# A hand-written order on TensorE: scores and conditioning chunks moved between a tile's transpositions and its value products

## Chip, cores and metric

The kernel runs on one core of one Trainium2 chip. The metric is the device time of one launch in microseconds (us). The engines are TensorE (PE in the profile, with its weight loads as PEld), VectorE (DVE), ScalarE (ACT), GpSimd (POOL) and SyncE (SP, which here only issues the loads of weights). Each engine works through its own list of instructions in the order of that list.

## What is computed

A model of two layers on 256 tokens of width 1024. Layer 0 mixes with a gated linear recurrence, layer 1 with an attention of three branches; each layer ends with a gated feed-forward part, and every part is scaled and shifted by columns computed from a conditioning vector `c`. The change lies in layer 1. Cut to what matters:

```python
mods = einsum('bd,lde->lbe', silu(c), ada_w) + ada_b        # shift, scale, gate of four parts
kc, vc = compress(k_cmp), compress(v_cmp)                   # silu(flat @ w1) @ w2, kc then normalised
q = rms_norm(h @ w_q, q_norm); q_rope = apply_rope(q)
o_c = softmax(mask(q @ kc)) @ vc                            # compressed branch
o_s = softmax(mask(q_rope @ ks)) @ vs                       # selected branch
o_w = softmax(mask(q_rope @ kw)) @ vw                       # window branch
y = (g0 * o_c + g1 * o_s + g2 * o_w) @ w_out
x = x + gate * y
```

## The kernel before

Weights come as 1 MB chunks in the fixed order `SCHED`, over the SP queue into four buffers (`raw`). A chunk of a projection is split by ACT (`wh`) and DVE (`wl`) into a high and a low part, and TensorE multiplies three times per product (`mm3`). A conditioning chunk (`ada_pe`, products `adapsg` for a gate, `adapsss` for shift and scale) is read by TensorE straight from `raw`. A buffer is loaded again once its reader is done.

The attention of layer 1 (`nsa`) is written as units, generators that issue some instructions and yield. `ORDER["nsa"]` is a list of their names; each word lets one unit go on to its next yield:

- `q0` to `q3`: a query projection (`nq`), then its rotation, for which four small transfers (`usq`) are issued from the ACT queue. `n0`, `n1`, `n2`: the norm of a pair of query chunks or of the keys: sums on TensorE (`hs`), a chain of small steps over ACT and DVE (`hry`, `hrt`, `hrr`), products that spread the result (`hb`), and the scaling on DVE (`QR`, `QN`).
- `c`: the compression, whose tail (`cmp_tail`) is a chain of small steps: transpositions (`hidt`), products (`kc`, `kcms`, `vc`), with DVE steps between. `G`: gates. `w0`, `w1`: the values (`v`). `x0`, `x1`: compressed softmax (`cs`, `css`, transposed as `pct` to `PC`).
- For each head tile j from 0 to 7: `s` (`attend_scores`) makes scores `s` on TensorE, DVE adds the mask and takes maxima into `Pt`, ACT takes eight exponentials in place, and DVE scales `Pt`. `p` (`attend_turns`) transposes `Pt` on TensorE into `ptt`, and DVE (one of four) and ACT (three of four) copy it to `PT`. `v` (`attend_values`) makes the output `po` from `PT` and the values, and ACT and DVE split it to `hh` and `hl`.
- `a`: the next conditioning chunk, of twelve: four of the gate of the attention, eight for the last feed-forward part. After the last chunk of each group ACT copies the sum (`adasm`), TensorE transposes it (`adat`), and DVE adds the bias.

In this stretch TensorE keeps exactly the order in which the units write (`InOrder` ties each product to the one before it). ACT and DVE are ordered by the scheduler from the dependences. Score tiles, `po`, `hb`, `adat` and other small results share four PSUM buffers (`m_tile`) taken in turn; `ptt` and the projections share three others (`acc_tile`). `Pt` has three buffers. After the attention come the output projection (`nso`), the second feed-forward part (`ff`, `ffo`), and the end.

Of the kernel before, what the change touches and what calls it, by code (L numbers as in the profile page):

```python
# [52 lines left out]
def _ada_g(l):  # L53
# [12 lines left out]
    "hada": [1, 1, 3, 4, 6, 6, 6, 7, 7, 7, 8, 8],  # L66
    "f0": [11, 11, 12, 12, 13, 17, 19, 20, 20, 20, 25, 25, 26, 27, 29, 30, 32, 33, 35, 36],
    "nsa": (
# [3 lines left out]
    ).split(),  # L72
    "f1": [15, 16, 24, 29],
}
# [151 lines left out]
class K:  # L226
# [177 lines left out]
    def ada_pe(self, kind, l, i, t):  # L404

        nc = self.nc
        ss = kind == "ss"
        q = 512 if ss else 256
        if i == 0:
            self.aps = self.pp.tile([P, 512], F32, tag="ada", bufs=1, name=f"adaps{kind}{l}")  # L410
        ks = [i] if ss else [2 * i, 2 * i + 1]
        last = i == (7 if ss else 3)
        for n, k in enumerate(ks):
            for j in range(4):
                self.pe.matmul(self.aps[32 * j:32 * j + 32, :q], lhsT=self.c32[:, k],
                                 rhs=t[:, n * D + j * q:n * D + (j + 1) * q], start=k == 0, stop=k == KD - 1,
                                 tile_position=(0, 32 * j))
        if not last:
            return
        m, A, bias = self.ada_tiles(l)  # L420
        nb = q // P
        sm = self.tp.tile([P, 512], F32, tag="junk", bufs=1, name="adasm")
        nc.scalar.copy(sm[:, :q], self.aps[:, :q])
        pt = self.m_tile([P, 4, P], "adat")
        for b in range(nb):
            self.pe.transpose(pt[:, b, :], sm[:, b * P:(b + 1) * P], self.c("ident"))
        lo, hi = (0, 16) if ss else (16, 24)
        nc.vector.tensor_tensor(m[:, lo:hi].rearrange("p (j b) -> p j b", b=nb),
                                pt.rearrange("p b (j r) -> p j b r", r=32)[:, :, :nb, 0],
                                bias[:, lo:hi].rearrange("p (j b) -> p j b", b=nb), op=ALU.add)  # L430
        if ss:
            nc.vector.scalar_tensor_tensor(A, m[:, 8:16], 1.0, self.col(self.gain(l)), op0=ALU.add, op1=ALU.mult)
            self.mods[("A", l)] = A
            self.mods[("shift", l)] = m[:, 0:8]
        else:
            self.mods[("gate", l)] = m[:, 16:24]
# [592 lines left out]
    def nsa(self):  # L1029
        nc = self.nc  # L1030
        with self.tc.tile_pool(name="ns", bufs=1) as sp, self.tc.tile_pool(name="ns2", bufs=2) as s2, \
# [85 lines left out]
            for t in ORDER["nsa"]:  # L1117
                n = int(t[1:] or 0)
                if t == "a":
                    self.adas(1)  # L1120
                    continue
                if t[0] == "v" and self.O is None:
                    self.O = self.h_tiles(0)
                if (t[0], n) not in units:
                    units[t[0], n] = make[t[0]](n)
                next(units[t[0], n], None)
# [351 lines left out]
```

## Time and profile before

| | |
|---|---|
| time, median of 3 runs | 772.63 us (771.39 to 773.84) |
| the profiled execution | 770.48 us, of which its span is 768.7 us |
| TensorE busy | 718.0 us, 93% of the span |
| DVE, ACT busy | 568.6 us (74%), 399.7 us (52%) |
| mean granted TensorE clock | 0.991 of full |

The span runs from the first to the last instruction of the profiled execution; the rest of its time lies around it. Busy times overlap between engines, and products are pipelined, so the idle time of an engine and what ended it say more than its busy share.

### The profile page before, as it was taken

Reading aid. Unit: us, or ns where it says so; the run is one execution under the profiler, and the core shown is the slowest. Engines: PE = TensorE matmul, PEld = TensorE weight load, DVE = VectorE, ACT = ScalarE, POOL = GpSimd, SP = SyncE. Lnnn points to the kernel's source line nnn. Section 1 sums busy time; section 2 is a strip of 40 time slices with the busy share of each in tenths; the row PEclk is TensorE's granted clock in tenths of the full one; section 3 lists DMA queues with packets and bytes.
Section 4 is the critical chain, followed back from the end, with each engine's and each line's share of the span. In section 5 each row is a group of like instructions: output and inputs, shape, how many; then the busy total and the mean of one; then the engine's idle time right before and its main releaser. Section 6 shows DMA issues by size and latency. Waiting matters only on the chain.

```text
span 768.7 us, 15837 instructions
## 1 busy us (share of the span) xinstructions
PE 718.0 (93%) x6548; PEld 663.5 (86%) x6548; DVE 568.6 (74%) x1167; ACT 399.7 (52%) x758; POOL 0.4 (0%) x5
## 2 busy tenths in 40 slices
PE   4999998899999999999998787878999999999997
PEld 2999976799999999999997766544699999999997
DVE  6996988378998979888697796664489758565531
ACT  4339877356635454545476545355476544444330
POOL 0000000000000000000000000000000000000000
PEclk9999999999999999999999998999999999999999
DMA  8999646457397978987545722026965555755710
GB/s 335 335 353 352 253 154 278 170 190 254 117 371 292 364 282 336 350 300 287 178 147 193 285 70 69 1 110 238 359 240 203 187 198 212 256 202 208 267 42 22
DMA packets 26571, 174.13 MB, mean 227 GB/s; under 512 B 3201, under 2 KB 4609, under 8 KB 6018
## 3 DMA queue, kind: packets, MB, share of 16 engines
q1 hardware_dynamic: 24912, 170.80, 60.0%
q10 hardware_dynamic: 1586, 2.32, 1.1%
q8 instruction: 51, 0.84, 0.4%
q14 instruction: 22, 0.18, 0.1%
HBM read 170.48 MB, written 1.05 MB: 223 GB/s over the span
## 4 chain that ended last, share of the span: by engine, by line
PE 79%; DVE 9%; ACT 6%; DMA 3%; issue 2%; ACTq 0%; DVEq 0%
PE ff L516 11%; PE ff L514 11%; PE ff L515 11%; PE ffo L514 6%; PE ffo L515 5%; PE ffo L516 5%; ACT Pt L459 3%; DVE wl L338 2%; PE po L220 1%; DVE Pt L1300 1%; PE s L220 1%; PE hg_g L514 1%; PE hg_i L796 1%; PE nso L514 1%; PE q L515 1%
## 5 line engine op out<-in xcount | busy, mean ns | idle before, releaser
L338 DVE TENSOR_TENSOR wl<-raw,wh 128x1024 fp32r<-128x1024 f32 x201 | 243.7, 1221 | 75.3 <-ACT wh L337 74.5
L337 ACT CAST wh<-raw 128x1024 fp32r<-128x1024 f32 x201 | 208.3, 1048 | 146.3 <-PE ff L515 53.0
L516 PE MATMUL ff<-hh,wl 128*128 128x256 f32 (+1 forms) x704 | 198.5, 282 | 0.0
L514 PE MATMUL ff<-hh,wh 128*128 128x256 f32 (+1 forms) x704 | 198.2, 282 | 0.0
L515 PE MATMUL ff<-hl,wh 128*128 128x256 f32 (+1 forms) x704 | 197.7, 281 | 0.0
L516 PEld LDWEIGHTS ff<-hh,wl 128*128 128x128 f32 x704 | 133.1, 189 | 0.0
L514 PEld LDWEIGHTS ff<-hh,wh 128*128 128x128 f32 x704 | 132.7, 189 | 0.3 <-ACT hh L550 0.2
L515 PEld LDWEIGHTS ff<-hl,wh 128*128 128x128 f32 x704 | 132.6, 189 | 0.0
L514 PE MATMUL ffo<-gh,wh 128*128 128x256 f32 x352 | 99.0, 282 | 0.6 <-DVE x L668 0.6
L515 PE MATMUL ffo<-gl,wh 128*128 128x256 f32 x352 | 98.6, 280 | 0.0
L516 PE MATMUL ffo<-gh,wl 128*128 128x256 f32 x352 | 98.5, 280 | 0.0
L389 DVE CUSTOM_DVE_ANT_0 junk<-raw,crep 128x1024 f32<-128x1024 f32 x64 | 78.0, 1219 | 1.3 <-DMA raw<-in_w 0.6
L514 PEld LDWEIGHTS ffo<-gh,wh 128*128 128x128 f32 x352 | 66.0, 188 | 1.3 <-DVE x L668 1.0
L516 PEld LDWEIGHTS ffo<-gh,wl 128*128 128x128 f32 x352 | 66.1, 188 | 0.0
L515 PEld LDWEIGHTS ffo<-gl,wh 128*128 128x128 f32 x352 | 66.1, 188 | 0.0
L509 ACT CAST gh<-fg 128x256 fp32r<-128x256 f32 x44 | 17.8, 405 | 41.5 <-DVE fg L957 40.9
L459 ACT ACTIVATE Pt<-Pt,nm 128x128 f32<-128x128 f32 x64 | 28.2, 443 | 18.1 <-DVE nm L1304 18.1
L510 DVE TENSOR_TENSOR gl<-fg,gh 128x256 fp32r<-128x256 f32 x44 | 18.5, 421 | 8.2 <-ACT gh L509 8.2
L617 ACT ACTIVATE hh<-t,mod 128x256 fp32r<-128x256 f32 x24 | 11.4, 505 | 24.0 <-DVE t L616 24.0
L459 ACT ACTIVATE fs<-ff 128x256 f32<-128x256 f32 x38 | 14.4, 380 | 14.9 <-PE ff L516 14.8
L668 DVE SCALAR_TENSOR_TENSOR x<-ffo,mod,x 128x256 f32<-128x256 f32 x16 | 7.7, 481 | 19.1 <-PE ffo L516 19.1
L220 PE MATMUL nq<-hh,wl 128*128 128x256 f32 x64 | 18.7, 292 | 1.0 <-DVE wl L338 1.0
(323 smaller groups left out, 1446.7 us busy)
## 6 DMA issues: line engine op xcount, KB each, us to landing
raw<-in_w SPq DMA_DIRECT2D x160, 1024.0 KB, 5.9
x<-in_x SPq DMA_DIRECT2D x2, 512.0 KB, 4.9
usq<-huq ACTq DMA_DIRECT2D x16, 64.0 KB, 2.0
out<-x SPq DMA_DIRECT2D x8, 128.0 KB, 2.1
cst<-in_cst ACTq DMA_DIRECT2D x1, 558.0 KB, 7.6
raw<-in_w SPq DMA_DIRECT2D x1, 512.0 KB, 3.5
usk<-huk ACTq DMA_DIRECT2D x8, 64.0 KB, 2.6
rselr<-in_rsel SPq DMA_DIRECT2D x1, 256.0 KB, 2.8
```

What stands on the lines that cost most here:

```text
L220: return self.then(self.k.nc.tensor.matmul(*a, **k))
L337: nc.scalar.copy(wh, u)
L338: nc.vector.tensor_tensor(wl, u, wh.bitcast(F32), op=ALU.subtract)
L389: nc.vector.tensor_tensor_reduce(out=junk, in0=t[:, h * D:(h + 1) * D], in1=self.crep, scale=1.0, scalar=0.0, op0=ALU.mult, op1=ALU.add, a ...
L459: r = nc.scalar.activation(out, in_, func, **kw)
L509: self.nc.scalar.copy(hi, v)
L510: self.nc.vector.tensor_tensor(lo, v, hi.bitcast(F32), op=ALU.subtract)
L514: mm(ps, lhsT=wh, rhs=hh, start=first, stop=False)
L515: mm(ps, lhsT=wh, rhs=hl, start=False, stop=False)
L516: return mm(ps, lhsT=wl, rhs=hh, start=False, stop=last)
L617: self.last_hh = nc.scalar.activation(hh[:, m, :256], t, AF.Identity, bias=sh[:, m:m + 1])
L668: nc.vector.scalar_tensor_tensor(xn[:, m], ps, gate[:, m:m + 1], xn[:, m], op0=ALU.mult, op1=ALU.add)
```

## The change

The list `ORDER["nsa"]` is written anew, and the tail of a conditioning group (`ada_cols`) becomes a word of its own, `A`.

```diff
     "nsa": (
-        "q0 q0 q0 q0 n2 c G G c G q1 q1 q1 c q1 c w0 w0 c c n0 w0 w0 q2 q2 q2 q2 n0 s0 s0 x0 s1 s1 q3 q3 x0 q3 q3 "
-        "s2 s2 n1 w1 w1 w1 w1 n1 p0 p0 v0 s3 s3 p1 p1 v1 s4 s4 x1 p2 p2 v2 s5 s5 a a x1 p3 p3 v3 s6 s6 a a p4 p4 v4 "
-        "s7 s7 a a a p5 p5 v5 a a p6 p6 v6 a a a p7 p7 v7"
+        "q0 q0 q0 q0 n2 c G G c G q1 q1 q1 q1 w0 w0 c w0 w0 n0 c q2 q2 c c q2 q2 n0 s0 s0 x0 s1 s1 q3 q3 q3 q3 s2 s2 "
+        "x0 n1 w1 w1 w1 w1 p0 p0 a n1 v0 s3 s3 p1 p1 s4 s4 v1 x1 p2 p2 s5 s5 v2 a x1 p3 p3 s6 s6 v3 a p4 p4 s7 s7 v4 "
+        "a A a p5 p5 a v5 a a p6 p6 a a v6 a a p7 p7 A v7"
     ).split(),
...
-        if not last:
-            return
+        if last and isinstance(self.pe, InOrder):
+            self.ada_tail = lambda: self.ada_cols(l, ss, q)
+        elif last:
+            self.ada_cols(l, ss, q)
+
+    def ada_cols(self, l, ss, q):
+        nc = self.nc
         m, A, bias = self.ada_tiles(l)
         nb = q // P
...
                 if t == "a":
                     self.adas(1)
                     continue
+                if t == "A":
+                    self.ada_tail()
+                    continue
```

On TensorE, the second norm of the queries. Before, its eight `hb` products (the last two are shown) follow the products of the values (`v`) directly, and the first tile's transpositions (`ptt` from `Pt`) and value products (`po`) come after them:

```order
L220 MATMUL hb<-hry,rsel 128x256
L220 MATMUL hb<-hrt,rsel 128x256
L223 MATMUL ptt<-cst,Pt_5727 128x128 x12
L220 MATMUL po<-PC_5855,VC 64x256 x2
L220 MATMUL po<-PT_10_6028,V 64x256
```

Now the transpositions and a first conditioning chunk stand between the last product of the values and the first two of `hb`:

```order
L220 MATMUL v_5958<-wh_1_5952,hl_5240 128x256
L223 MATMUL ptt<-cst,Pt_5727 128x128 x12
L220 MATMUL adapsg_6032<-raw_5526,c_110 32x256 x8
L220 MATMUL hb<-hry,rsel 128x256
L220 MATMUL hb<-hrt,rsel 128x256
```

So `hb` moved behind two pieces of work that do not need it.

On TensorE, tile 1 (`Pt_5783`). Before, its values (`po`, ten products) follow its transpositions, and the scores come behind:

```order
L223 MATMUL ptt<-cst,Pt_5783 128x128 x12
L220 MATMUL po<-PC_5855,VC 64x256 x2
L220 MATMUL po<-PT_10_6103,V 64x256
L220 MATMUL po<-PT_00_6097,V 64x256
L220 MATMUL po<-PT_10_6103,V 64x128
L220 MATMUL po<-PT_00_6097,V 64x128
L220 MATMUL po<-PT_11_6115,V 64x256
L220 MATMUL po<-PT_01_6109,V 64x256
L220 MATMUL po<-PT_11_6115,V 64x128
L220 MATMUL po<-PT_01_6109,V 64x128
L220 MATMUL s_6138<-KR,QR 128x256
```

Now the scores of tile 4 stand between the two:

```order
L223 MATMUL ptt<-cst,Pt_5783 128x128 x12
L220 MATMUL s_6136<-KR,QR 128x256
L220 MATMUL s_6135<-KR,QR 128x256
L220 MATMUL s_6144<-KR,QR 128x512
L220 MATMUL s_6143<-KR,QR 128x512
L220 MATMUL po<-PC_5927,VC 64x256 x2
L220 MATMUL po<-PT_10_6114,V 64x256
```

The same holds for tiles 2, 3 and 4 with the scores of tiles 5, 6 and 7.

On ACT, the copy `adasm` after the gate's last chunk. Before, it stands behind the last exponential of tile 5 and ahead of the copies of tile 4:

```order
L459 ACTIVATE Pt_6328,sm<-Pt_6328,nm 128x128
L459 ACTIVATE Pt_6328,sm<-Pt_6328,nm 128x256
L423 COPY adasm<-adapsg_6263 128x256
L1338 COPY PT_10_6394<-ptt 128x384
L1338 COPY PT_01_6400<-ptt 128x384
```

Now it stands behind the last exponential of tile 7 and ahead of the copies of tile 5:

```order
L464 ACTIVATE Pt_6398,sm<-Pt_6398,nm 128x128
L464 ACTIVATE Pt_6398,sm<-Pt_6398,nm 128x256
L428 COPY adasm<-adapsg_6032 128x256
L459 ACT_TABLE_LOAD
L1346 COPY PT_10_6474<-ptt 128x384
```

So the copy moved two tiles back on ACT; on TensorE `adat` still follows the gate's last chunk directly.

## Rows read from the trace of the kernel before

**Rows 1.** The page: busy time of each engine, share of the span, instructions.

```profile
PE 718.0 (93%) x6548; PEld 663.5 (86%) x6548; DVE 568.6 (74%) x1167; ACT 399.7 (52%) x758; POOL 0.4 (0%) x5
```

**Rows 2.** Two stretches: length, busy time of each engine, clock, DMA share, GB/s.

```profile
422.00:551.00 129.00, 103.55 (x784) 72.83 (x783) 83.70 (x276) 65.03 (x202) 0.00 (x0) 0.96 0.42 154
551.00:768.70 217.70, 213.71 (x1780) 212.35 (x1779) 136.68 (x205) 98.57 (x148) 0.00 (x0) 1.00 0.53 189
```

**Rows 3.** TensorE's waits, 422 to 551 us: total, times, longest.

```profile
PE po L220 <- ACT PT L1338: 7.0, 4, 2.8
PE adat L223 <- ACT adasm L423: 4.0, 2, 3.3
PE pct L223 <- DVE nm L1304: 3.6, 1, 3.6
PE hb L220 <- ACT hry L509: 3.4, 1, 3.4
PE hidt L223 <- DVE hid L1185: 1.8, 1, 1.8
PE kc L220 <- DVE wd L1203: 1.5, 1, 1.5
...
PE ptt L223 <- ACT PT L1338: 0.8, 3, 0.3
PE hs L220 <- DVE mx L1300: 0.6, 1, 0.6
PE adapsss L220 <- DMA raw<-in_w: 0.6, 1, 0.6
```

**Rows 4.** Waits of DVE and ACT in the same stretch.

```profile
ACT Pt L459 <- DVE nm L1304: 18.1, 6, 4.0
DVE rs L1313 <- ACT Pt L459: 17.9, 7, 3.7
...
DVE usq L1002 <- DMA usq<-huq: 2.5, 1, 2.5
DVE VC L1229 <- PE vc L220: 2.3, 1, 2.3
```

**Rows 5.** Groups by line, 422 to 551 us: busy, mean ns of one, idle before.

```profile
L1300 DVE CUSTOM_DVE_ANT_0 Pt<-s,cst 128x128 f32<-128x128 f32 (+1 forms) x64 | 18.9, 351 | 0.2 <-PE s L220 0.2
L1321 DVE TENSOR_TENSOR Pt<-Pt,cf 128x768 f32<-128x768 f32 x16 | 14.6, 953 | 0.2
L338 DVE TENSOR_TENSOR wl<-raw,wh 128x1024 fp32r<-128x1024 f32 x12 | 14.4, 1214 | 1.7 <-ACT wh L337 1.6
```

**Rows 6.** Instructions of TensorE in order of time: start, us.

```profile
504.00 0.65 PE L220 MATMUL po<-PT,V 128*64 128x256 f32 x4 [2.77 <-ACT PT L1338]
...
522.16 0.44 PE L223 MATMUL adat<-cst,adasm 128*128 128x128 f32 x2 [3.34 <-ACT adasm L423]
...
538.31 1.74 PE L223 MATMUL ptt<-cst,Pt 128*128 128x128 f32 x12
...
549.96 0.87 PE L220 MATMUL po<-PT,V 128*64 128x256 f32 x8
```

**Rows 7.** Four stretches, columns as in Rows 2.

```profile
462.00:464.00 2.00, 2.00 (x10) 2.00 (x10) 1.24 (x2) 2.00 (x11) 0.00 (x0) 0.50 0.16 20
480.00:482.00 2.00, 2.00 (x12) 2.00 (x12) 2.00 (x4) 0.00 (x0) 0.00 (x0) 0.53 0.00 0
504.00:506.00 2.00, 2.00 (x14) 1.15 (x14) 2.00 (x6) 0.37 (x1) 0.00 (x0) 1.00 0.00 0
524.00:526.00 2.00, 2.00 (x10) 1.16 (x11) 0.76 (x3) 1.04 (x3) 0.00 (x0) 0.50 0.57 234
```

**Rows 8.** The chain that ended last, whole run: start, us, what.

```profile
518.24 3.61 ACT Pt L459 x16
...
530.87 2.29 ACT Pt L459 x11
...
536.52 1.04 PE adapsss L220 x8
```

## Prediction

> **What bounds the kernel now.** I read the page first: TensorE is busy for 718.0 of 768.7 us and no other engine comes near [rows 1]. So time can only come out of stretches in which TensorE stands still. The table of stretches shows where: from 422 to 551 us, the attention, it is busy for 103.6 of 129.0 us; from 551 us to the end for 213.7 of 217.7 us [rows 2]. The part behind the attention starts when the attention ends and is then bound by TensorE, so what the attention saves comes off the end at full value. The third view, the waits of TensorE in this stretch, names what is to be had: 25.2 us over thirteen groups, of which the nine that the argument needs are shown [rows 3], and the difference of the two numbers above, 25.4 us, agrees. That is the ceiling for idle time, and the change touches nearly every line of it.
>
> The fourth view says why it can't all go. The largest waits of the other two engines are a pair: ACT waits 18.1 us for DVE's `nm`, and DVE waits 17.9 us for ACT's exponentials [rows 4]. The reader is to see a loop: maxima, exponentials (3.6 us a tile [rows 8]), scaling of `Pt` (2 x 0.95 us), and 8 maxima of 0.35 us each before the next `nm` [rows 5]. Each list is run in order, so a new order on TensorE helps only as far as this loop and the other lists let it.
>
> Finally the clock. After the waits of 3.4 us (`hb`) and 3.3 us (`adat`) the granted clock is 0.53 and 0.50, the 1.2 GHz level, and after that of 3.6 us (`pct`) 0.50, while after one of 2.8 us it is 1.00 [rows 3, 6, 7].
>
> **The change, step by step.** Nothing is added or removed in work: the same products, copies and transfers in another order. I read the new lists of TensorE, ACT and DVE side by side and put the durations of the rows to them. Each term is what TensorE waits before, less what it waits after.
>
> T1, compression's tail. Before, `hidt` and `kc` wait 1.8 and 1.5 us [rows 3]; now 24 products of the values stand ahead of each, and both waits go. But the query norm `n0` and the first scores need DVE's list, and there only the wait for `vc` (2.3 us) goes; that for the transfer `usq` (2.5 us) stays, and waits for ACT come to it [rows 4]. About 2 us of idle time reappear ahead of `hb`. I take 1.0 us of gain; bounds 0 and 3.3.
>
> T2, `pct`. Before, `x0`'s transposition stands 24 query products behind the scores and waits 3.6 us, and `hs` behind it 0.6 us [rows 3]. Now all 48 query products and the scores of tile 2 stand ahead of it, and its softmax is ready. What is late next: the last `wl` of the value weights `w1` stands on DVE behind the maxima of tile 2 and costs 1.2 us [rows 5], and the second dozen value products need it. Gain 4.2 - 1.2 = 3.0 us; bounds 2.0 and 4.2.
>
> T3, `hb` of `n1`. Before it waits 3.4 us for the last step of the chain on ACT and DVE [rows 3]. Now 12 transpositions (1.74 us [rows 6]) and a chunk (1.04 us [rows 8]) stand ahead of it. But on ACT the chain now stands behind the exponentials of tiles 1 and 2, with four issues of `usq` among them, and behind the copy of the values; on DVE it stands behind the scaling of two tiles. The chain comes about 1 us earlier than before, and TensorE, early by T1 and T2 less these 2.8 us, too: the wait stays at about 3.4 us. And the third of the transpositions' four PSUM tiles now waits about 1.2 us for the copy of the values to free a buffer. Net -1.2 us; bounds -1.5 and +3.4 (the chain in time).
>
> T4, the value products of tiles 1 to 4. Before, `po` waits 7.0 us for copies of `ptt`, and `ptt` 0.8 us [rows 3]: ACT runs eight exponentials between the copies. The four score products now ahead of `po` (about 2 us) cover most of this for tiles 1 and 3 and half of it for tile 4. For tile 2 another wait takes its place. The small PSUM tiles go round in fours, so `po` of tile 2 needs the buffer of tile 5's first scores, which DVE reads only after the scaling of tile 4 (2 x 0.95 us) and among eight steps of `x1`: 2.4 us, and 0.9 us ahead of it, where these scores wait for `hl` of tile 1, behind eight exponentials. Sum after: 0.5 + 2.4 + 0.9 + 0.9 + 0.4 = 5.1 us, gain 7.8 - 5.1 = 2.7 us; bounds 0 and 7.
>
> T5, `adat`. Before it waits 3.3 us for `adasm`, behind the exponentials of tile 5 (begun at 518.24, 3.61 us [rows 8]), and 0.7 us at the second group: 4.0 in all [rows 3]. Now `A` follows the last gate chunk with nothing between, and ACT has `adasm` behind the exponentials of tile 7. Their start, by the loop above, is about 517 us, their end 521; TensorE arrives at about 517. I take 4.2 us. The second `A` has 12 transpositions ahead of it and costs nothing. Net -0.2 us; bounds -3 and +4.0. The Trainium skill says in TensorE: Matmul & The Clock Gate, section Architectural detail, that ACT and DVE take their queue strictly in order while TensorE can only pull weight loads ahead. By that rule `adasm` can't overtake the exponentials and the 4.2 us stand; if it could, the sum would be about 4 us better. The trace agrees: 518.24 + 3.61 is 521.85, and `adat` starts at 522.16 [rows 6, 8].
>
> T6, transfers. The first chunk is used at about 473 us in place of 507, so its buffer is loaded again 34 us sooner, and chunks 5 to 12 follow, each one buffer round behind. The last two still come close together with tile 6 and 7, and the output projection's weights queue behind them on SP: I take 1.8 us (1.3 for the last chunk, 0.5 at the first `nso`) against 0.6 before [rows 3]. Net -1.2 us; bounds -3 and +0.6.
>
> T7, the clock. Three slow stretches before, each about 3.4 us at half speed, so about 1.7 us apiece; with `pct` gone two are left (`hb`, `adat`). Gain 1.7 us; bounds 0 and 5.1. The Trainium skill, same page, section HAM oscillation, states that long idle gaps send the array back to half rate and that work must be laid so that it stays warm. By that rule the price hangs on these two waits alone: the 3.4 us still to be had are lost as long as they stay. The rows shown agree with it.
>
> Sum: 1.0 + 3.0 - 1.2 + 2.7 - 0.2 - 1.2 + 1.7 = 5.8 us. A second way, without the ledger: in the new order `adat` and, behind it, eight chunks (8 x 1.04), three tiles of transpositions (3 x 1.74) and of values (3 x about 2 us; the last 8 of 20 rows take 0.87 [rows 6]) and the second `adat` follow the wait that ends at 521.3 us: about 20.5 us, with 1.7 for the clock and 1.3 for the transfer 544.8 us. Before, the last value product ends at 549.96 + 0.87 = 550.83 us [rows 6]: 6.0 us. I take 6.0 us: 770.48 - 6.0 = 764.5 us for the profiled execution. It lies 2.15 us under the median of the runs, so the median becomes 772.6 - 6.0 = 766.6 us. A difference of 0.3%, about 2.3 us, is what a measurement can tell from none.
>
> **The rivals.**
>
> The waits only move. TensorE is ahead of the loop of DVE and ACT, and whatever stands earlier is waited for later: T4 gives 0, T2 2.0, T7 0, the rest as above: 1.0 + 2.0 - 1.2 - 0.2 - 1.2 = 0.4 us. For it: the pair of 18 us [rows 4]. Against: DVE is busy only for 83.7 and ACT for 65.0 of 129 us [rows 2]. Time 772.2 us.
>
> The cover is better than I read. `adasm` is in time, or the chain of `n1` is: either gives 4 to 5 us and its slow stretch of 1.7 us, so 12 us in all: 760.6 us. For it: 2.8 us of work ahead of `hb`. Against: both are behind exponentials on ACT's list.
>
> Slower, by `adat`. It stands between the last gate chunk and everything else that TensorE has left, and behind the exponentials of tile 7 in place of tile 5. If the new order brings these no sooner than before (530.87 us [rows 8]), `adat` starts at 534.8, the 20.5 us behind it end at 555.3 and, with the transfer then in time and the clock as before, 4.5 us are lost: 777.1 us. It decides from a start of about 526 us on; I expect 517. Against: the scores of tiles 3 to 7 all stand earlier among TensorE's products, and the waits of T2 alone move them 3 us.
>
> **How the numbers follow.** The forecast has 0.60, the better cover 0.20, waits that only move 0.13, slower 0.07. The forecast's own bounds, most terms not at their ends at once, are 762 to 770 us. The range to hold 8 in 10 takes in the better cover down to 759.5 and part of the moved waits up to 771.5 us. Faster by over 0.3% (under 770.3): all of the better cover and nearly all of the forecast, 0.79. Same: 0.14. Slower: 0.07.
>
> **What would show it.** T1: no waits at `hidt` and `kc`, one of about 2 us at `hb` of `n0`. T2: none at `pct`, about 1 us inside `v`. T3: `hb` of `n1` starts at about 477 us after 3.5 us, the clock then near 0.5. T4: `po` of tile 2 waits for DVE, not for ACT's copies. T5: one wait of about 4 us at the first `adat` for `adasm`, with exponentials until about 521 us. The end of the last `po` at 544 to 545 us, and a part behind it as long as before. Wrong it would be made by a wait on none of these places, or by an `nso` that starves for weights.

## The result and the profile after

The new order takes 769.02 us, the median of nine runs (766.25 to 772.83), against 774.19 us for the kernel before, run between them (nine runs, 771.39 to 776.76). The ratio is 0.9933, with a 95% interval of 0.9906 to 0.9959: 5.2 us faster, where 6.0 us were forecast. The profiled execution takes 767.16 us (forecast 764.5), its span is 765.4 us.

The page's busy line of the new kernel, which answers to [rows 1]: the work of TensorE is the same, at a lower mean clock (0.984 against 0.991).

```profile
PE 719.0 (94%) x6548; PEld 664.1 (87%) x6548; DVE 567.9 (74%) x1167; ACT 399.0 (52%) x758; POOL 0.4 (0%) x5
```

Two stretches of the new kernel, as in [rows 2]: the attention, and all behind it.

```profile
422.00:545.00 123.00, 102.15 (x762) 71.91 (x762) 81.01 (x271) 62.04 (x200) 0.00 (x0) 0.92 0.43 153
545.00:765.40 220.40, 216.01 (x1802) 213.89 (x1798) 138.58 (x210) 100.45 (x150) 0.00 (x0) 1.00 0.53 192
```

As the prediction has it, the gain lies in the attention; but the granted clock there fell from 0.96 to 0.92, where it should have risen. The waits of TensorE, 422 to 551 us, which answer to [rows 3]:

```profile
PE hb L220 <- ACT hry L514: 5.0, 1, 5.0
PE adat L223 <- ACT adasm L428: 3.8, 1, 3.8
PE vc L220 <- DVE hrt L495: 3.0, 1, 3.0
PE po L220 <- DVE mx L1308: 2.0, 1, 2.0
PE po L220 <- ACT PT L1346: 1.9, 2, 1.0
PE v L220 <- DVE wl L338: 1.1, 1, 1.1
...
PE adapsss L220 <- DMA raw<-in_w: 1.0, 1, 1.0
PE ptt L223 <- DVE PT L1344: 0.8, 2, 0.5
...
PE ptt L223 <- ACT PT L1346: 0.2, 1, 0.2
```

Gone are `pct`, `hidt`, `kc` and most of the wait of `po` for the copies. In their place stand a longer wait of `hb` (5.0 for 3.4), one of `vc` (3.0) that I had put elsewhere, and the forecast ones: `po` for the maxima of tile 2, `wl` inside `v`, the last transfer.

The waits of ACT and DVE, 422 to 545 us, which answer to [rows 4]:

```profile
ACT hh L514 <- PE po L220: 19.5, 6, 6.3
...
ACT Pt L464 <- DVE nm L1312: 6.0, 3, 3.8
...
DVE rs L1321 <- ACT Pt L464: 4.0, 3, 3.4
```

The pair that stood at 18.1 and 17.9 us fell to 6.0 and 4.0 us; ACT now waits most for `po` of TensorE. So the loop of maxima and exponentials, which the prediction takes as the limit of any new order, held this order far less than the old one. Both e1 (13.6 and 14.6 us) and e2 (11.0 and 8.2 us), described below, have part of the fall.

To see where the time went, I cut the attention at a point that both kernels pass with nearly the same work done, the start of tile 3's scores behind `hb`. It begins where the gates are transposed (`gt`) and ends with the last `po`. Each profile has its own start, so lengths are compared. First before, then after, columns as above:

```profile
421.75:484.97 63.22, 50.06 (x365) 43.02 (x365) 49.58 (x136) 31.69 (x87) 0.00 (x0) 0.95 0.38 131
484.97:550.83 65.86, 53.57 (x421) 29.89 (x419) 34.10 (x140) 33.47 (x114) 0.00 (x0) 0.97 0.46 177
```

```profile
421.69:486.10 64.41, 53.02 (x382) 44.07 (x380) 49.34 (x136) 30.74 (x87) 0.00 (x0) 0.89 0.43 145
486.10:546.70 60.60, 51.14 (x403) 29.31 (x401) 33.09 (x139) 33.30 (x114) 0.00 (x0) 0.94 0.46 168
```

The front, up to tile 3's scores, became 1.2 us longer, the back 5.3 us shorter; 1.04 us of each is the one chunk that moved from back to front. Idle time, length less TensorE's busy time, fell from 13.2 to 11.4 us in front and from 12.3 to 9.5 us in the back, 4.6 us in all. Busy time, less the chunk, rose by 1.9 us in front and fell by 1.4 us in the back, though the products are the same. In front that is the clock, 0.89 for 0.95. The fall in the back, at a clock of 0.94 for 0.97, needs another cause; e9 below shows half of it in the scores. The sum, 4.1 us, less 0.8 us that the part behind the last `po` is longer in this profile, is the 3.3 us between the two profiled executions. The medians differ by more, 5.2 us: the profile shown of before is one of its fastest executions (770.48 us at a clock of 0.991, where runs of before have a median near 0.982).

### The profile page after: what moved, and what is told of

Its sections match the earlier page's. It is cut to its first block, busy times and chain, and to the rows that moved or that the text cites. A ratio compares the mean times of both kernels' runs of the same rounds, so it can differ in the third digit from the quotient of the medians.

```text
span 765.4 us, 15842 instructions
## 1 busy us (share of the span) xinstructions
PE 719.0 (94%) x6548; PEld 664.1 (87%) x6548; DVE 567.9 (74%) x1167; ACT 399.0 (52%) x758; POOL 0.4 (0%) x5
## 5 line engine op out<-in xcount | busy, mean ns | idle before, releaser
L622 ACT ACTIVATE hh<-t,mod 128x256 fp32r<-128x256 f32 x24 | 11.4, 505 | 24.4 <-DVE t L621 24.4
L1308 DVE CUSTOM_DVE_ANT_0 Pt<-s,cst 128x128 f32<-128x128 f32 (+1 forms) x64 | 19.4, 351 | 5.6 <-PE s L220 5.6
L464 ACT ACTIVATE fs<-ff 128x256 f32<-128x256 f32 x38 | 14.4, 380 | 14.6 <-PE ff L521 14.6
```

The lines of the kernel that those rows point to most:

```text
L464: r = nc.scalar.activation(out, in_, func, **kw)
L622: self.last_hh = nc.scalar.activation(hh[:, m, :256], t, AF.Identity, bias=sh[:, m:m + 1])
L1308: nc.vector.tensor_tensor_reduce(out=Pt[half][:, br, o:o + n], in0=ps[half][:, br], in1=cs[:, S - n:], scale=1.0, scalar=-3e38, op0=ALU.ad ...
```

## The experiments

Twelve runs, each timed beside the kernel before on the same chip. Except where it is said, the edit is one of the written order alone. The table gives the ratio to before; the median of the mean granted clock over the runs of a kernel (before had 0.979 to 0.982 in these jobs); and from its profile the length from `gt` to the last `po` and TensorE's idle time in it. Filler products count as busy.

| kernel | ratio (95%) | median clock | length | idle |
|---|---|---|---|---|
| before | 1 | 0.979 to 0.982 | 129.1 | 25.5 |
| after | 0.9933 (0.9906 to 0.9959) | 0.982 | 125.0 | 20.9 |
| e1 new front, old back | 1.0033 (1.0007 to 1.0060) | 0.979 | 133.4 | 26.1 |
| e2 old front, new back | 0.9852 (0.9822 to 0.9881) | 0.991 | 122.5 | 19.0 |
| e3 after, old compression tail | 0.9918 (0.9889 to 0.9947) | 0.983 | 122.6 | 21.1 |
| e4 after, `hb` of `n1` later | 0.9825 (0.9799 to 0.9850) | 0.984 | 119.2 | 14.6 |
| e5 e3 and e4 together | 0.9815 (0.9777 to 0.9854) | 0.989 | 119.2 | 15.9 |
| e6 e5, `A` later | 0.9822 (0.9781 to 0.9862) | 0.989 | 117.4 | 15.7 |
| e7 after, filler ahead of `hb` | 0.9879 (0.9845 to 0.9912) | 0.984 | 123.9 | 16.0 |
| e8 after again | 0.9916 (0.9889 to 0.9944) | 0.982 | 128.2 | 21.0 |
| e9 before, scores moved | 0.9894 (0.9858 to 0.9930) | 0.985 | 124.1 | 20.3 |
| e10 before, chunks and `n1` moved | 0.9924 (0.9897 to 0.9951) | 0.985 | 126.6 | 23.2 |
| e11 e5, filler ahead of `adat` | 0.9761 (0.9727 to 0.9795) | 0.995 | 116.2 | 11.5 |
| e12 e5 with the front of before | 0.9805 (0.9772 to 0.9838) | 0.989 | 120.1 | 16.7 |

The ratios are to be trusted first, the idle column second, the length last, since it holds the clock of one execution: the changed kernel, profiled twice (after and e8), has the same idle time, 20.9 and 21.0 us, and the same waits within 0.7 us each, but lengths of 125.0 and 128.2 us.

**Front and back apart.** e1 keeps the new order up to the values (`w1`) and goes back to the old one behind it, the conditioning tail included. e2 is the reverse:

```diff
 e1, behind w1 (the lines of before return):
-p0 p0 a n1 v0 s3 s3 p1 p1 s4 s4 v1 ... v4 a A a p5 p5 a v5 a a p6 p6 a a v6 a a p7 p7 A v7
+n1 p0 p0 v0 s3 s3 p1 p1 v1 s4 s4 ... v4 s7 s7 a a a p5 p5 v5 a a p6 p6 v6 a a a p7 p7 v7
 e2, ahead of w1 (the lines of before return):
-q1 q1 q1 q1 w0 w0 c w0 w0 n0 c q2 q2 c c q2 q2 n0 s0 s0 x0 s1 s1 q3 q3 q3 q3 s2 s2 x0 n1
+q1 q1 q1 c q1 c w0 w0 c c n0 w0 w0 q2 q2 q2 q2 n0 s0 s0 x0 s1 s1 q3 q3 x0 q3 q3 s2 s2 n1
```

> The new order up to the value products w1 (compression's tail and x0 moved), the old one from the first transpositions on. Theory A: the front's savings are eaten by the wait for hb of n1, whose chain on ACT and DVE comes no earlier; so the first scores of tile 3 start within 1 us of before (484.97 us) and the time is that of before within 1.5 us (ratio 0.998 to 1.002). Rival B: the tail and pct give 2 to 4 us that last to the end (ratio 0.995 to 0.997).

> The old order up to w1, the new one from the first transpositions on (scores ahead of the value products, chunks spread, the late A). Theory A: all of the gain of the changed kernel is here, 4 us or more at the end of the last value product, ratio 0.992 to 0.995. Rival B: half of it, ratio 0.996 to 0.998.

Measured: e1 is 0.3% slower than before, e2 1.5% faster, more than either of its expectations had. The front takes from the change rather than adding to it. The longest wait of TensorE in e1, 422 to 551 us:

```profile
PE hb L220 <- ACT hry L509: 7.9, 1, 7.9
```

It was 3.4 us before [rows 3]: the waits removed at `pct` and the compression are all met again here, and at `vc` (2.5 us).

**Which half of the front.** e3 gives the changed kernel the old compression tail back and leaves `x0` where the change put it. It differs from e2 only in the place of `x0`:

```diff
-q1 q1 q1 q1 w0 w0 c w0 w0 n0 c q2 q2 c c q2 q2 n0 s0 s0 x0
+q1 q1 q1 c q1 c w0 w0 c c n0 w0 w0 q2 q2 q2 q2 n0 s0 s0 x0
```

> The changed kernel with the old order of compression's tail (q1 to n0), all else new. Theory A: the new tail gave nothing, since the wait for the transfer usq on DVE decides there; the first scores start at about 448.5 us in place of 449.1, and the time is that of the changed kernel or up to 1 us less (ratio 0.991 to 0.994). Rival: the tail was worth the 3.3 us of its two waits, and the time goes back by 2 to 3 us (ratio 0.996 to 0.998).

Measured: no difference from the changed kernel that the runs can tell (0.9918; after had 0.9933 and, timed again as e8, 0.9916), so the tail is worth nothing that they show either way: `hidt` and `kc` wait 1.8 and 1.5 us again, `vc` no longer waits. Against e2 (0.9852) it is slower, and the intervals do not meet. So what costs is the move of `x0`. The two profiles show this only in part. `hb` waits 4.7 us here and 0.9 us in e2, where `pct` and `hs` wait 3.1 us instead, and the idle times differ by 2.1 us; the lengths are alike, since the profile of e3 is the fastest of its runs and that of e2 the slowest. The rest of the 4.8 us between the medians goes with the clock (0.983 for 0.991), and how `x0` sets that is not shown.

Why `hb` waits longer, the chain that ended last in the changed kernel shows (start, us, what):

```profile
469.62 6.37 DMA usq<-huq
476.11 0.75 DVE usq L1007
476.94 0.65 DVE QR L1008
477.59 1.74 DVE Pt L1329 x2
479.32 0.34 DVE hrt L495
...
480.02 0.43 DVE hrr L498
480.54 0.41 ACT hry L514
480.99 2.32 PE hb L220 x8
```

The chain of `n1` stands on DVE behind `usq` and two scalings of `Pt`, and `usq` is a transfer that took 6.37 us. The view of the tile `usq` gives the time from issue to landing, first for e2, then for e3, 440 to 486 and 440 to 482 us:

```profile
DMA to landing us min/median/max: 2.0/2.0/2.1
```

```profile
DMA to landing us min/median/max: 2.0/3.3/6.5
```

Beside the transfer stands a load of weights, issued on SP's queue (changed kernel, 468 to 475 us):

```profile
468.73 0.33 SPq L317 DMA_DIRECT2D raw<-in_w  x1
```

The four `usq` transfers of 64 KB are issued from ACT's queue at 467.73, 468.34, 468.98 and 469.62 us. The first two landed after 2.0 us; the last two, issued just behind a load of 1 MB, after 6.8 and 6.4 us. The next load is issued at 476.05 us, when they have landed. In before, the load is issued at 462.98 us, 4.1 us ahead of the first `usq`, and `usq` finds the way free. From e2 to e3, in which only `x0` moves, the first `usq` comes 3.5 us earlier behind `gt` and the load 1.6 us later, and so they meet. In all nine kernels profiled with `x0` moved the longest `usq` takes 6.2 to 7.0 us, and in the five with `x0` in its old place 2.1 to 3.3 us (before, e2, e9, e10, e12). The Trainium skill says in DMA: Bandwidth & Descriptors, section Issuing engines are not separate DMA queues, that transfers of different engines run on the same 16 DMA engines and interleave; these rows agree.

The transfer is not all of the wait. DVE stood idle for this `usq` for 1.7 us in the changed kernel (1.5 us in e3, 4.0 us in e1) and not at all in before and e2. So an estimate from these rows is that 1.7 us of the 5.0 us of `hb` are the transfer's. The rest is TensorE's early arrival at a chain that came no earlier: `hb` starts 56.7 us behind `gt` in before and in e3, and 59.3 us in the changed kernel. No run moves the load or the transfer alone.

**`hb` later.** If `hb` waits for a chain that comes no earlier, it should stand later. e4 moves it behind tile 0's values, the scores of tile 3 and half of tile 1's transpositions. e5 is e4 with the old tail of e3, e12 is e5 with the whole old front, `x0` included:

```diff
 e4:
-p0 p0 a n1 v0 s3 s3 p1 p1 s4 s4 v1
+p0 p0 a v0 s3 s3 p1 n1 p1 s4 s4 v1
```

> The changed kernel with the second half of n1 (its hb products) moved behind the value products of tile 0, the scores of tile 3 and half of the transpositions of tile 1. Theory A: the wait for hb of 5.0 us is a chain on ACT and DVE that five more us of work cover; the wait falls under 1.5 us, its slow stretch of the clock goes, and the time falls by 3 to 6 us against the changed kernel (ratio 0.985 to 0.990). Rival: the wait moves on, to the scores of tile 4, which need this norm, and less than 1 us is won (ratio 0.992 to 0.995).

> The changed kernel with the old order of compression's tail and with the second half of n1 moved behind the scores of tile 3 and half of the transpositions of tile 1, that is both of the single edits that kept or won time. Theory: the two don't meet on TensorE (one ends at the first scores, the other begins at hb), so their gains add: 1 us of the first and 8 us of the second against the changed kernel, ratio to before 0.978 to 0.984. Rival: both only shift the same wait on DVE's list, and it is no better than the second alone, 0.981 to 0.986.

> The whole front of before, its x0 included, with the later hb half of n1 and the rest as in the best order so far (0.9815). It tells what moving x0 alone is worth once hb no longer waits. By my step T2: pct waits again, 3.6 us or a little less, and its slow stretch of 1.5 us is back, less 1 us inside v: 2 to 4 us more than that order, ratio 0.984 to 0.987. Rival: what pct waits is taken off the adat wait behind it, since both stand ahead of the same loop of DVE and ACT, and it stays within 1 us: 0.9805 to 0.983.

Measured: 0.9825 for e4, 0.0108 below the ratio of the changed kernel; somewhat more than was expected; no wait at `hb` is left, one of 1.3 us at scores appears. e5 (0.9815) and e12 (0.9805) can't be told from it. So with `hb` out of the way the place of `x0` is worth nothing that the runs can tell; the rival named for e12 held. Its waits at `pct` (1.7 us), `hs` (2.0) and the compression return, and its `adat` starts 97.4 us behind `gt` where it starts 96.1 us in e5: most of what is waited for early is waited for anyway.

**Scores or chunks.** e9 is the kernel before with only the scores of tiles 4 to 7 moved, e10 the old front with only the chunks, `A` and `n1` moved:

```diff
 e9, against before:
-p1 p1 v1 s4 s4 x1 p2 p2 v2 s5 s5 a a x1 p3 p3 v3 s6 s6 a a p4 p4 v4 s7 s7
+p1 p1 s4 s4 v1 x1 p2 p2 s5 s5 v2 a a x1 p3 p3 s6 s6 v3 a a p4 p4 s7 s7 v4
 e10, against e2:
-p1 p1 s4 s4 v1 x1 p2 p2 s5 s5 v2 a x1 p3 p3 s6 s6 v3 a p4 p4 s7 s7 v4 a A
+p1 p1 v1 s4 s4 x1 p2 p2 v2 s5 s5 a x1 p3 p3 v3 s6 s6 a p4 p4 v4 s7 s7 a A
```

> The order of before, with one thing moved: the scores of tiles 4 to 7 stand between the transpositions and the value products of tiles 1 to 4. Front, n1, chunks and the conditioning tail as before. My step T4 put 2.7 us on this move (bounds 0 and 7), with the wait of po for ACT's copies falling from 7.0 to about 3 us and one of about 2 us for the maxima taking its place: ratio to before about 0.9965. Rival: the whole of the back part gave 0.985 by itself (about 11 us), and if it is the scores that bring it, this kernel comes to 0.987 or below. Third way: the scores alone give nothing, since the adat wait grows by what is won, 1.000.

> The other half: the front of before up to the values, then the scores behind a tile's value products as before, but the chunks spread singly, the late conditioning tail, and hb of n1 behind the first tile's transpositions and a chunk. If the gain of the back part (about 11 us together) is a sum of parts, this kernel gains what the kernel with moved scores alone does not: about 6 to 8 us, ratio about 0.990, with hb waiting about 1 us and the clock slow behind adat only. Rival: without the scores ahead, po waits 7 us for copies as before and adat waits longer (tile 7's exponentials come later), and it stays at 0.998 to 1.003.

Measured: 0.9894 and 0.9924; the gains, 8.2 and 5.9 us, add to 14.1 where both together (e2) gave 11.5. So each half wins time by itself. The sum can't be told from the 11.5 us, since each ratio is known to about 0.3%, nor the scores alone (0.9894) from the whole change (0.9933). The interval of e9 leaves out both the 0.9965 of my step T4 and its third way, 1.000. Some waits of e9, 422 to 551 us:

```profile
PE adat L223 <- ACT adasm L423: 4.6, 2, 3.9
PE ptt L223 <- ACT PT L1338: 2.0, 2, 1.7
...
PE po L220 <- DVE mx L1300: 2.0, 1, 2.0
...
PE po L220 <- ACT PT L1338: 1.0, 1, 1.0
```

`po` and `ptt` together fall from 7.8 us [rows 3] to 5.0, as T4 has it. In e10 `po` waits 9.7 us, and nothing of `adat` is left but 0.5: without the scores ahead, TensorE meets the same work of ACT one place earlier. What e10 gains comes in front of tile 3's scores (60.7 us from `gt` for 63.2 before, with a chunk more), where `hb` waits 0.9 us; behind them it takes 65.8 us, as long as before with a chunk less.

In e9 the same stretch takes 60.1 us in place of 65.9. Only 2.6 us of the 5.7 are idle time (12.3 to 9.7); the rest is time in which TensorE counted as busy. The groups by line in this stretch show half of it in the scores themselves (busy, mean ns, idle before), first in before, then in the changed kernel:

```profile
L220 PE MATMUL s<-KR,QR 64*128 64x256 f32 (+1 forms) x40 | 11.7, 522 | 0.0
```

```profile
L220 PE MATMUL s<-KR,QR 64*128 64x256 f32 (+1 forms) x40 | 9.5, 514 | 0.0
```

Forty products of nearly the same mean length cover 2.2 us less (9.9 us in e9, so 1.8 less; the 13.2 us of e10 hold slower products, of 643 ns). The waits of the weight loads (PEld), 422 to 551 us, account for 1.4 us of it. Before, then after:

```profile
PEld s L220 <- DVE hl L510: 2.5, 5, 0.9
```

```profile
PEld s L220 <- DVE hl L515: 1.1, 2, 0.8
```

Where the scores follow `po`, their loads wait five times for DVE's `hl`, the last reader of the PSUM buffer of an earlier `po`; the waits of the products (PE) don't list it. Ahead of their tile's `po` they wait twice, in e9 too (1.1 us). What makes up the rest is not shown.

The idle column must be read with that in mind, and with another thing that e9 shows: its front is that of before, yet has 10.6 us of idle time in place of 13.2, at a clock of 0.89 in place of 0.95 and 0.7 us longer. The order is the same, so the reading is that slow products ahead of a wait use the wait up.

**`adat` and the clock.** e6 takes e5 and lets `A` follow tile 5's values, so that TensorE has work while `adasm` is on its way:

```diff
-v4 a A a p5 p5 a v5 a a p6 p6
+v4 a p5 p5 v5 A a a a a p6 p6
```

> As the kernel before it in this list, and the first A moved behind the transpositions and values of tile 5, the chunks of the last group behind it. Theory: the wait of about 4 us at the first adat is for exponentials that stand ahead of adasm on ACT, and 3.7 us of other products cover it: the wait at adat falls under 1 us and the time by 2 to 4 us. Rival: the values of tile 5 then wait for the same exponentials, or the chunks, used later, wait longer for their transfers (now about 1 us), and less than 1 us is won.

Measured: 0.9822, no gain over e5. The wait of 4.2 us at `adat` is gone, but two others of TensorE, 1.2 and 1.4 us in e5, have grown (422 to 545 us):

```profile
PE adapsss L220 <- DMA raw<-in_w: 3.5, 2, 2.0
PE po L220 <- ACT PT L1346: 3.4, 3, 2.0
```

The idle time is the same, 15.7 us for 15.9. e7 and e11 leave the waits and fill them. e7 puts 36 products of 256 columns, whose result is overwritten, into `hb`'s own buffer ahead of the changed kernel's `hb`; e11 puts 34 of them into `adat`'s buffer in e5. All outputs are still computed.

```diff
 e11, in ada_cols:
         pt = self.m_tile([P, 4, P], "adat")
+        if isinstance(self.pe, InOrder) and not ss:
+            for _ in range(34):
+                self.pe.matmul(pt[:, 0:2], lhsT=self.rsel[:, 0:P], rhs=self.fill_rhs, start=True, stop=True)
```

> The changed kernel with 36 products of 256 columns added ahead of the hb products of n1, in a buffer that hb then overwrites: TensorE works on nothing useful for some 4.3 of the 5.0 us in which it waits there. Theory on the clock: the slow stretch behind this wait (hb's eight products 2.32 us, the values of tile 0 2.93 us, against 1.1 and 1.95 at full clock) comes from the idle time, so it goes, and the scores of tile 3 start 2 us earlier; time 1.5 to 2.5 us less than the changed kernel. Rival: the clock there hangs on something else, or DVE's list sets the scores anyway; the time is that of the changed kernel or up to 1 us more.

> The best order so far (tail of the compression as before, hb half of n1 later: 0.9815) with 34 products that compute nothing used ahead of the first adat, into its own buffer, so that TensorE works while adasm is waited for. The output stays that of the reference. If the slow stretch behind adat is the price of the idle time, adat still starts about where it did and the chunks behind it run at full clock: 1.5 to 2.5 us less than that order, ratio about 0.979. If the clock falls there for another reason, or elsewhere instead, nothing or a loss of up to 1 us: 0.9815 to 0.983.

> The changed kernel unchanged, beside the three others on their chip. If the slow stretches of the clock belong to the order of the work, they stand at the same five places as in its first profile (about 445, 455, 481, 503 and 527 us); if they also hang on chance, one or more moves or goes while the waits stay the same. Time ratio 0.991 to 0.996.

e8, the changed kernel unchanged in the job of e7, gave 0.9916; e7 gave 0.9879, and each of its six runs (762.18 to 766.38 us) is faster than each of the nine of e8 (766.59 to 771.16 us). The slow stretches of e8 begin near the five places expected, but the second lasts about twice as long as in the first profile, and the fourth begins 3 us earlier. TensorE around `hb`, first after, then e7 (start, us; the wait in brackets):

```profile
480.99 0.58 PE L220 MATMUL hb<-hry,rsel 128*128 128x256 f32 x1 [5.00 <-ACT hry L514]
...
483.24 1.12 PE L220 MATMUL po<-PC,VC 128*64 128x256 f32 x4
484.15 2.02 PE L220 MATMUL po<-PT,V 128*64 128x256 f32 x16
486.10 1.12 PE L220 MATMUL s<-KR,QR 64*128 64x256 f32 x5
```

```profile
475.78 4.37 PE L220 MATMUL hb<-hh,rsel 128*128 128x256 f32 x36
480.97 0.39 PE L220 MATMUL hb<-hry,rsel 128*128 128x256 f32 x1 [0.82 <-ACT hry L514]
...
482.45 0.65 PE L220 MATMUL po<-PC,VC 128*64 128x256 f32 x4
482.94 1.47 PE L220 MATMUL po<-PT,V 128*64 128x256 f32 x16
484.34 2.12 PE L220 MATMUL s<-KR,QR 64*128 64x256 f32 x8
```

`hb` starts at the same time, but `po` comes 0.8 us and the scores 1.8 us earlier, since the clock is not lowered: it is 1.00 from 478 to 486 us, for 0.57 in the changed kernel. e11 shows the same at `adat`, and more of it. The stretch from `adat` to the last `po` in e5, then in e11:

```profile
517.34:540.53 23.19, 22.03 (x167) 11.15 (x167) 6.00 (x15) 8.44 (x15) 0.00 (x0) 0.86 0.79 308
```

```profile
516.77:536.86 20.09, 19.31 (x167) 9.83 (x167) 5.98 (x16) 8.34 (x15) 0.00 (x0) 1.00 0.87 340
```

`adat` starts 96.1 us behind `gt` in both, so the filler delays nothing. The same 167 products then take 3.1 us less: 2.7 us less busy at a clock of 1.00 in place of 0.86, and 0.4 us less idle. The ratio, 0.9761, is 0.0054 or some 4.2 us below that of e5, of another job, where 1.5 to 2.5 us were expected, and the median clock is 0.995. The intervals of the two ratios still meet, so the gain over e5 rests on this stretch of the two profiles more than on the runs. e11 has the lowest ratio of all, 756.86 us against 775.46 for before in its job, and 1.7% under the changed kernel as it was first timed.

## Why the prediction was right, and where its steps were not

The time was right, and so was the mechanism as a whole: waits are removed from TensorE, several come back elsewhere, and what the attention saves comes off the end. The rival of moved waits (772.2 us, from the idle time of before) describes the front alone, not the sum. But the parts came otherwise than their terms, two errors met, and so the time is in part luck.

- **T1**, compression's tail, 1.0 us of gain: mis-sized. `hidt` and `kc` no longer wait, but the 2 us that I put ahead of `hb` of `n0` are 3.0 us at `vc`, whose PSUM buffer a sum of the norm holds until DVE, waiting for a `usq` transfer, has read it. Worth nothing by e3.
- **T2**, `pct`, 3.0 us: the waits were as forecast (none at `pct`, 1.1 us inside `v`). But that this is a gain of the whole was the step that fell. With `x0` moved TensorE reached `hb` ahead of its chain, a weight load fell among the `usq` transfers that the chain waits for, and the wait returned at `hb`.
- **T3**, `hb`: I forecast a wait of 3.4 us and a start at 477 us; it waited 5.0 us and started at 480.99. I had named the issues of `usq` on ACT's list, but priced the transfer at nothing, from the profile of before, in which it runs alone; 1.7 us of the wait are its own by the estimate above. The 1.2 us that I put at the transpositions ahead were 0.3. T1 to T3 together were to take 2.8 us of idle time from the front and took 1.8 (13.2 to 11.4).
- **T4**, value products: 5.1 us of waits left were forecast, 4.9 were measured, `po` of tile 2 waiting 2.0 us for the maxima as named. So the idle part of the term, 2.7 us, was right (2.9, and 2.8 in e9). Its worth was larger: 5.7 us of the stretch in e9's profile, in part since the scores' own waits for `hl` fall as well, which the waits of TensorE's products don't list. e9 by its runs won 8.2 us, with the median clock at 0.985 for 0.979.
- **T5**, `adat`: forecast 4.2 us, measured 3.8, and none at the second group. The end of the chain shows why it cannot be sooner:

```profile
521.13 3.61 ACT Pt L464 x16
524.74 0.26 ACT adasm L428
525.05 0.44 PE adat L223 x2
```

`adasm` follows tile 7's sixteen pieces of exponentials without a gap, as T5 has it. They ended 3.7 us later than my 521 us, and `hb` was late by about as much (480.99 for 477 us); their start, 521.13 us, lies about halfway between my 517 and the 526 us from which the slower rival decides. From `adat` to the end of the last `po` 21.7 us passed, 23.5 were forecast.
- **T6**, transfers: 1.8 us forecast, 1.0 measured at the last chunk and no `nso` that starves.
- **T7**, the clock, 1.7 us of gain: wrong in sign. Half speed was to be left behind `hb` and `adat` alone. That there are three such stretches before was read from one execution, of a high clock: four other kernels with the same front (e2, e9, e10, e12) have one that begins between 451 and 457 us, ahead of `pct`, which then waits 1.5 to 2.6 us in place of 3.6. The clock of the new kernel in four stretches:

```profile
454.00:458.00 4.00, 4.00 (x17) 2.32 (x17) 3.12 (x14) 2.95 (x14) 0.00 (x0) 0.57 0.07 16
...
478.00:486.00 8.00, 5.01 (x28) 3.64 (x28) 5.41 (x10) 0.40 (x1) 0.00 (x0) 0.57 0.26 109
502.00:506.00 4.00, 3.19 (x20) 2.23 (x20) 2.76 (x17) 0.00 (x0) 0.00 (x0) 0.57 0.00 0
...
526.00:530.00 4.00, 4.00 (x28) 2.62 (x20) 1.75 (x4) 1.74 (x4) 0.00 (x0) 0.57 0.60 184
```

The second and the fourth are those of `hb` and `adat`. The first comes with no long wait just ahead of it (TensorE is busy throughout), the third with a wait of 1.97 us in it; a fifth lies behind `vc`, at 444 to 448 us. The Trainium skill, TensorE: Matmul & The Clock Gate, section HAM oscillation, speaks of long idle gaps; e7 and e11 agree, since filling such a gap kept the clock at 1.00, but the first stretch is none of these. In front busy time rose by 1.9 us, where T7 has a gain of 1.7.

So the idle terms sum to 4.1 us of gain and 4.6 were measured, with the front 1.0 us short and the back 1.5 us over; busy time, which T7 wanted 1.7 us lower, rose by 0.5 us, although it fell by 1.4 us in the back. By the two profiles the gain is then 3.3 us, about half of the forecast. The median of the runs fell by 5.2 us, nearer to the forecast than its terms deserve: by e1 the front alone costs 2.5 us, where T1 to T3 have a gain of 2.8, and by e2 the back alone wins 11.5, where T4 to T6 have 1.3.

What stays open: why the clock falls at 454 us without a long wait. It does so from a point between 451 and 457 us in every kernel but before and e3, and in the shown profile of before it falls later instead, at 461 us, in the wait of `pct`. In e9 it cost little, since `pct` then waited 1.5 us in place of 3.6. Ahead of it, in the changed kernel, TensorE has waits of 0.9 us in all among the first scores, then sixteen small products of `x0` (1.97 us); e3 has the same products there and kept its clock. What either does to the clock was not tried. e9's gain is 8.2 us by its runs and 5.0 us by the stretch of its profile; how much of the difference is the clock of single executions stays open too.

## What to carry to other kernels

A wait that is removed ahead of a chain of two other engines comes back at the next product that needs the chain: first ask what sets the chain's own time, and move the product that needs it rather than the work ahead of it (e4: 0.0108 of the time for one word of the order). A new order on one engine also shifts transfers against each other, and a large load can fall among small transfers that another chain waits for (6.2 to 7.0 us in place of 2.1 to 3.3). Where a wait of several us can't be avoided, filling it with products keeps TensorE's clock at full for the work behind it (3.1 us for 34 products).

## What the runs showed of the hardware

- Transfers of 64 KB from ACT's queue landed after 2.0 us alone, and after up to 7.0 us with one load of 1 MB issued on SP just ahead of them.
- With 34 products of 256 columns in the wait of 4.2 us ahead of `adat`, the clock of the stretch behind it (20 us) was 1.00; with TensorE idle in that wait it was 0.86 (23 us).
- The same program's lower clock lies in different places from one execution to the next: in the second profile of the changed kernel one slow stretch stands at 499 to 503 us in place of 502 to 506, and the mean clock of the attention is 0.89 in place of 0.92, with the same idle time. Runs of before span 1.1% in one job (769.64 us at a clock of 0.989, 777.74 us at 0.976), so differences of less than 0.3% need many runs.
